# The last layer norm of a two-layer trunk: GpSimd arithmetic taken out, half of one scaling given to TensorE, six held weight units in place of five

## The chip, the cores and the metric

The kernel runs on one core of one Trainium2 chip. The metric is the device time in microseconds (us) of one execution; a lower time is better.

## The reference, cut to what matters

The reference is a decoder trunk of two layers over 256 tokens of width 2048, in float32. Each layer is a mixer (several kinds of attention), a layer norm, a squared-ReLU MLP and a second layer norm. Only the very end matters here: the second matrix of the last MLP, the residual sum and the last layer norm, whose result is the output.

```python
def layer_norm(x, g, b):
    mu = jnp.mean(xf, axis=-1, keepdims=True)
    xc = xf - mu
    var = jnp.mean(xc * xc, axis=-1, keepdims=True)
    y = xc * lax.rsqrt(var + LN_EPS) * g + b
...
def sqrelu_mlp(x, w1, w2):
    hid = jax.nn.relu(jnp.einsum('bsd,df->bsf', x, w1))
    return jnp.einsum('bsf,fd->bsd', hid * hid, w2)
...
x = layer_norm(ALPHA * x + sqrelu_mlp(x, mlp_w1[layer], mlp_w2[layer]), ln2_g[layer], ln2_b[layer])
```

## The kernel before, in words

Nearly the whole run is one stream of weight units. A unit is 128 x 1024 float32 numbers (512 KB) that SyncE's queue loads from HBM; ScalarE casts it to a high part (`w_hi`, line 120) and VectorE subtracts that to get the low part (`w_lo`, line 121). TensorE multiplies both parts with the activations, three products for each 128 x 512 piece (lines 371 to 373). The order of work on each engine is the order in which the Python code issues it; no scheduler moves anything.

The 256 tokens lie as two groups of 128 partitions, t = 0 and t = 1, in the tile `x` (`x_res` in the trace), 2048 columns each. A function works on four column blocks c = 0 to 3 of 512.

`as_` computes one column block of an MLP's output for both token groups into two PSUM banks (`acc`). The last block of the last MLP is 8 units of 12 products each, 6 for either group. With `hold=5` the first three units are used for both groups at once, and the last five are held: TensorE first takes all five for t = 0 (30 products), which completes t = 0, and then all five again for t = 1. Four of the held units lie in the ring buffers of `w_hi` and `w_lo`; the last two units of the stream have tiles of their own (`end_hi`, `end_lo`).

`moments` adds the last block to `x` (line 558), takes the statistics of it on VectorE (`bn`, `mv`, `ve`: lines 560, 582, 569) and has GpSimd compute the reciprocal deviation `rs` as a power (line 571), for t = 0 and then for t = 1.

`final` is the last layer norm. `rows` (`gb_rows`) holds the gain and the bias, broadcast to all partitions. For each group it normalises blocks 0 and 2 on ScalarE (`(x - mean) * r`, as an affine function with the tile `nmr`), then multiplies with the gain and adds the bias in two further steps (`two`), the adds on GpSimd, the products on VectorE except one that GpSimd has too. Blocks 1 and 3 are done by VectorE alone, in two fused steps of three operands each (`one`, lines 654 and 655). Each finished block goes to HBM from SyncE's queue, 256 KB each, eight in all.

Of the kernel before, what the change touches and what calls it, by code (L numbers as in the profile page):

```python
# [11 lines left out]
F32 = mybir.dt.float32  # L12
F32R = mybir.dt.float32r
BF16 = mybir.dt.bfloat16
AF = mybir.ActivationFunctionType
ALU = mybir.AluOpType
AX = mybir.AxisListType

P = 128
# [144 lines left out]
class Trunk:  # L164
# [479 lines left out]

    def final(self, last, stats):

        nc = self.nc
        rows = self.rows
        ov = self.a["out"][0].rearrange("(t p) d -> p t d", p=P)

        def one(t, c, mv, r):
            cs = slice(c * 512, (c + 1) * 512)
            xb = self.x[:, t, cs]
            nc.vector.scalar_tensor_tensor(xb, xb, mv[:, 0:1], rows[:, 0, cs], op0=ALU.subtract, op1=ALU.mult)
            nc.vector.scalar_tensor_tensor(xb, xb, r[:, 0:1], rows[:, 1, cs], op0=ALU.mult, op1=ALU.add)
            nc.sync.dma_start(ov[:, t, cs], xb)

        def two(t, c, op):
            cs = slice(c * 512, (c + 1) * 512)
            xb = self.x[:, t, cs]  # L660
            if op == ALU.mult:
                (nc.vector if t or c else nc.gpsimd).tensor_tensor(xb, xb, rows[:, 0, cs], op=op)
            else:
                nc.gpsimd.tensor_tensor(xb, xb, rows[:, 1, cs], op=op)
                nc.sync.dma_start(ov[:, t, cs], xb)

        for t, (mv, r) in enumerate(self.moments(last, stats)):
            nm = self.small.tile([P, 1], F32, name="nmr")
            nc.vector.scalar_tensor_tensor(nm, mv[:, 0:1], -1.0, r[:, 0:1], op0=ALU.mult, op1=ALU.mult)
            for c in (0, 2):  # L670
                xb = self.x[:, t, c * 512:(c + 1) * 512]
                nc.scalar.activation(xb, xb, AF.Identity, bias=nm, scale=r[:, 0:1])
            one(t, 1, mv, r)
            two(t, 0, ALU.mult)
            two(t, 0, ALU.add)
            two(t, 2, ALU.mult)
            two(t, 2, ALU.add)
            one(t, 3, mv, r)


    def qk(self, sc, q, k):
# [389 lines left out]
    def mlp(self, layer):  # L1071
        nc = self.nc
        st = self.new_stats()
        for q in range(4):
            hs = []
            cur = {}

            def take(f, bank):
                if f % 2 == 0:
                    cur["r"] = self.mp.tile([P, 512], F32, name="relu", bufs=3)  # L1080
                r = cur["r"]
                self.join(r[:, (f % 2) * S:(f % 2) * S + S], bank)
                if f % 2 == 0:
                    return
                sq = self.mp.tile([P, 512], F32, name="sq", bufs=2)
                hh = self.mp.tile([P, 512], F32R, name="h_hi", bufs=12)
                hl = self.mp.tile([P, 512], F32R, name="h_lo", bufs=12)

                def square():
                    nc.scalar.activation(r, r, AF.Relu)  # L1090
                    nc.scalar.activation(hh, r, AF.Square)
                    nc.vector.tensor_tensor(sq, r, r, op=ALU.mult)
                    nc.vector.tensor_tensor(hl, sq, hh.bitcast(F32), op=ALU.subtract)

                self.late.append(square)
                for j in range(2):
                    hs.append((hh[:, j * S:(j + 1) * S], hl[:, j * S:(j + 1) * S], None))

            for b in range(4):
                self.ws(self.xT, KT, 512, take, more=b % 2 == 1)  # L1100
                self.pump()
            self.finish_side()
            if layer == DEPTH - 1 and q == 0:
                self.rows = self.gb_rows(2, layer)
            for c in range(4):
                end = q == 3 and c == 3
                o = self.as_(hs, 16, 512, hold=(5 if layer else 2) if end else 0)
                if not end:
                    self.add_res(o, c, q == 0, st if q == 3 else None)
        return (o, c, False), st  # L1110
# [54 lines left out]
```

## Time and profile before

| What | us |
|---|---|
| median of 3 runs | 2243.89 |
| lowest and highest of them | 2241.61, 2249.12 |
| the profiled execution, its own time | 2248.41 |
| span of the profiled execution, first to last instruction | 2246.6 |

The span is what the trace shows; the profiled execution's own time is 1.81 us longer than its span. In the trace PE is TensorE, PEld its weight loads, DVE VectorE, ACT ScalarE, POOL GpSimd, and SPq the queue on which SyncE issues transfers. All times inside the trace count from the start of the span.

### The profile page before, as it was taken

What the parts mean: (1) busy time and instruction counts of PE and PEld (TensorE: products, weight loads), DVE (VectorE), ACT (ScalarE), POOL (GpSimd) and SP (SyncE); (2) the same over time, 40 slices, a digit from 0 to 9 for tenths busy, and PEclk for the clock granted to TensorE, in tenths of its full rate; (3) what the DMA queues carried; (4) which work ended last, traced back from release to release, by engine and by line L of the source; (5) the groups of instructions that cost most, each with busy time, mean ns of one, the idle gap of its engine ahead of it and who ended that gap; (6) DMA issues with size and microseconds to landing.
All of it is one profiled execution on the core that took longest, in us unless ns stands there. A gap on an engine that the chain in (4) does not pass through costs nothing.

```text
span 2246.6 us, 30036 instructions
## 1 busy us (share of the span) xinstructions
PE 2216.6 (99%) x11604; PEld 1847.6 (82%) x11604; DVE 1406.8 (63%) x1903; ACT 1060.7 (47%) x1525; POOL 62.0 (3%) x85
## 2 busy tenths in 40 slices
PE   9999999999999999999999999999999999999997
PEld 7878887788888888888878887778888888888885
DVE  5766355776556456556567887978555655554655
ACT  4554344454345345345344575635434534444542
POOL 0000000000000000000003201000000000000001
PEclk9999999999999999999999999999999999999998
DMA  7444454555655556565658443455656556555652
GB/s 266 145 118 147 131 168 141 189 178 193 191 187 188 190 176 200 193 188 170 206 161 226 154 136 127 148 184 184 227 194 189 178 198 189 186 194 181 194 190 104
DMA packets 224320, 399.07 MB, mean 178 GB/s; under 512 B 12778, under 2 KB 56512, under 8 KB 223408
## 3 DMA queue, kind: packets, MB, share of 16 engines
q1 hardware_dynamic: 221760, 387.30, 54.2%
q0 software_dynamic: 2416, 9.84, 1.6%
q8 instruction: 91, 1.49, 0.3%
q14 instruction: 53, 0.43, 0.1%
HBM read 395.00 MB, written 2.10 MB: 177 GB/s over the span
## 4 chain that ended last, share of the span: by engine, by line
PE 64%; issue 30%; DVE 4%; ACT 1%; DMA 1%; POOL 0%; SPq 0%; POOLq 0%; DVEq 0%; ACTq 0%
PE acc L325 14%; PE acc L371 9%; PE acc L373 9%; PE acc L372 9%; PE acc L326 7%; PE sc L325 3%; PE sc L326 2%; PE o L325 2%; PE pt L325 2%; PE pt L259 1%; PE o L278 1%; PE sc L685 1%; DVE w_lo L121 1%; PE sc L684 1%; PE o L326 1%
## 5 line engine op out<-in xcount | busy, mean ns | idle before, releaser
L121 DVE TENSOR_TENSOR w_lo<-raw,w_hi 128x1024 fp32r<-128x1024 f32 (+2 forms) x748 | 891.5, 1204 | 600.0 <-ACT w_hi L120 595.0
L120 ACT CAST w_hi<-raw 128x1024 fp32r<-128x1024 f32 (+2 forms) x748 | 759.9, 1029 | 770.2 <-PE acc L373 460.9
L325 PE MATMUL acc<-x,w_hi 128*128 128x512 f32 x1824 | 654.0, 402 | 4.3 <-DVE x L514 4.0
L326 PE MATMUL acc<-x,w_lo 128*128 128x256 f32 x1824 | 512.3, 281 | 0.6 <-DVE w_lo L121 0.6
L325 PEld LDWEIGHTS acc<-x,w_hi 128*128 128x128 f32 x1824 | 343.3, 188 | 94.4 <-issue 6.6
L373 PE MATMUL acc<-w_hi,h_lo 128*128 128x512 f32 x1016 | 400.3, 394 | 0.0
L372 PE MATMUL acc<-w_lo,h_hi 128*128 128x512 f32 x1016 | 398.2, 392 | 0.0
L371 PE MATMUL acc<-w_hi,h_hi 128*128 128x512 f32 x1016 | 394.4, 388 | 0.0
L326 PEld LDWEIGHTS acc<-x,w_lo 128*128 128x128 f32 x1824 | 345.2, 189 | 1.4 <-DVE w_lo L121 0.9
L372 PEld LDWEIGHTS acc<-w_lo,h_hi 128*128 128x128 f32 x1016 | 190.7, 188 | 44.3
L371 PEld LDWEIGHTS acc<-w_hi,h_hi 128*128 128x128 f32 x1016 | 190.7, 188 | 42.7
L373 PEld LDWEIGHTS acc<-w_hi,h_lo 128*128 128x128 f32 x1016 | 191.0, 188 | 38.1
L325 PE MATMUL sc<-x,w_hi 128*128 128x512 f32 x512 | 186.7, 399 | 0.0
L326 PE MATMUL sc<-x,w_lo 128*128 128x256 f32 x512 | 143.8, 281 | 0.0
L371 PE MATMUL acc<-w_hi,x 128*128 128x256 f32 (+2 forms) x400 | 136.4, 341 | 0.3 <-DVE x L513 0.2
L373 PE MATMUL acc<-w_hi,x 128*128 128x256 f32 (+2 forms) x400 | 132.5, 331 | 0.0
L372 PE MATMUL acc<-w_lo,x 128*128 128x256 f32 (+2 forms) x400 | 132.4, 331 | 0.0
L325 PEld LDWEIGHTS sc<-x,w_hi 128*128 128x128 f32 x512 | 96.2, 188 | 23.9
L337 ACT ACTIVATE xfull<-acc 128x256 f32<-128x256 f32 x130 | 49.6, 383 | 126.2 <-PE acc L326 108.7
L326 PEld LDWEIGHTS sc<-x,w_lo 128*128 128x128 f32 x512 | 96.7, 189 | 0.0
L325 PE MATMUL o<-x,w_hi 128*128 128x512 f32 x256 | 96.3, 399 | 0.0
L325 PE MATMUL pt<-x,w_hi 128*128 128x512 f32 x256 | 96.2, 399 | 0.0
(203 smaller groups left out, 2163.9 us busy)
## 6 DMA issues: line engine op xcount, KB each, us to landing
raw<-in_mlp_w SPq DMA_DIRECT2D x512, 512.0 KB, 4.2
raw<-in_even_w_in SPq DMA_DIRECT2D x92, 512.0 KB, 4.4
raw<-in_odd_w_in SPq DMA_DIRECT2D x56, 512.0 KB, 4.1
raw<-in_odd_w_out SPq DMA_DIRECT2D x32, 512.0 KB, 3.7
raw<-in_even_w_out SPq DMA_DIRECT2D x24, 512.0 KB, 3.7
gb_rows<-in_ln_g POOLq DMA_DIRECT2D x3, 1024.0 KB, 5.0
gb_rows<-in_ln_b POOLq DMA_DIRECT2D x3, 1024.0 KB, 7.1
raw<-in_odd_w_uq SPq DMA_DIRECT2D x8, 384.0 KB, 4.7
```

Of the source, the lines that this page charges most:

```text
L120: nc.scalar.copy(h, r)
L121: nc.vector.tensor_tensor(l, r, h.bitcast(F32), op=ALU.subtract)
L259: nc.tensor.transpose(pt[:, b * P:(b + 1) * P], st[:, u * 384 + b * P:u * 384 + (b + 1) * P], self.ident)
L278: nc.tensor.matmul(o[rows, :], v, w[:, 0:S], start=first, stop=False, skip_group_check=True)
L325: nc.tensor.matmul(banks[f], hi[:, c:c + P], both, start=first, stop=False, skip_group_check=True)
L326: nc.tensor.matmul(banks[f][:, S:2 * S], lo[:, c:c + P], xh, start=False, stop=last, skip_group_check=True)
L337: nc.scalar.activation(t, bank[:, S:2 * S], AF.Copy, scale=scale)
L371: nc.tensor.matmul(outs[t], xh[:, ts], hi[:, c:c + width], start=first, stop=False, skip_group_check=True)
L372: nc.tensor.matmul(outs[t], xh[:, ts], lo[:, c:c + width], start=False, stop=False, skip_group_check=True)
L373: nc.tensor.matmul(outs[t], xl[:, ts], hi[:, c:c + width], start=False, stop=last, skip_group_check=True)
L684: nc.tensor.matmul(sc[:, 0:P], q[:, 0:P], k[:, 0:P], start=True, stop=True, skip_group_check=True)
L685: nc.tensor.matmul(sc[:, P:384], q[:, P:S], k, start=True, stop=True, skip_group_check=True)
```

## The change

`final` is written anew, and `hold` is 6 for the last block. GpSimd keeps only the power for `rs`. For t = 0 all four blocks are done by VectorE in two fused steps, `centre` (subtract the mean, multiply with the gain) and `scale` (multiply with `r`, add the bias). For t = 1 blocks 2 and 3 are done the same way. Blocks 0 and 1 of t = 1 are centred by VectorE, and the scaling is a product on TensorE: ScalarE makes a diagonal matrix `dr` (tile name `g_row`) of `r`, one product with the identity puts the bias into a PSUM bank, a second with `dr` adds the scaled block, ScalarE copies the bank back and issues the transfer from its own queue. All operands of these products are float32.

```diff
-        for t, (mv, r) in enumerate(self.moments(last, stats)):
-            nm = self.small.tile([P, 1], F32, name="nmr")
-            nc.vector.scalar_tensor_tensor(nm, mv[:, 0:1], -1.0, r[:, 0:1], op0=ALU.mult, op1=ALU.mult)
-            for c in (0, 2):
-                xb = self.x[:, t, c * 512:(c + 1) * 512]
-                nc.scalar.activation(xb, xb, AF.Identity, bias=nm, scale=r[:, 0:1])
-            one(t, 1, mv, r)
-            two(t, 0, ALU.mult)
-            two(t, 0, ALU.add)
-            two(t, 2, ALU.mult)
-            two(t, 2, ALU.add)
-            one(t, 3, mv, r)
+        def centre(t, c, mv):
+            xb, _, g, _ = cut(t, c)
+            nc.vector.scalar_tensor_tensor(xb, xb, mv[:, 0:1], g, op0=ALU.subtract, op1=ALU.mult)
+
+        def scale(t, c, r):
+            xb, o, _, b = cut(t, c)
+            nc.vector.scalar_tensor_tensor(xb, xb, r[:, 0:1], b, op0=ALU.mult, op1=ALU.add)
+            nc.sync.dma_start(o, xb)
+
+        banks = [self.ps.tile([P, 512], F32, name=n) for n in ("pt", "o")]
+        dr = self.small.tile([P, P], F32, name="g_row", bufs=3)
+        for t, (mv, r) in enumerate(self.moments(last, stats)):
+            if t:
+                nc.scalar.activation(dr, self.ident, AF.Copy, scale=r[:, 0:1])
+                for c, bank in enumerate(banks):
+                    nc.tensor.matmul(bank, self.ident, cut(t, c)[3], start=True, stop=False, skip_group_check=True)
+            centre(t, 0, mv)
+            centre(t, 1, mv)
+            for c in range(2):
+                if t:
+                    xb, o, _, _ = cut(t, c)
+                    nc.tensor.matmul(banks[c], dr, xb, start=False, stop=True, skip_group_check=True)
+                    nc.scalar.copy(xb, banks[c])
+                    nc.scalar.dma_start(o, xb)
+                else:
+                    scale(t, c, r)
+            for c in range(2, 4):
+                centre(t, c, mv)
+                scale(t, c, r)
...
-                o = self.as_(hs, 16, 512, hold=(5 if layer else 2) if end else 0)
+                o = self.as_(hs, 16, 512, hold=(6 if layer else 2) if end else 0)
```

VectorE's order for t = 1, from the statistics to the program's end, was this (line 558 adds the last block, 662 is the gain of `two`, 654 and 655 are `one`):

```order
L558 TENSOR_TENSOR x_res<-x_res,acc 128x512 [waits PE_49]
L560 BN_STATS bn_13460<-x_res 128x6 [waits DVE_49]
L582 BN_AGGR mv<-bn_13460 128x2 [waits DVE_49]
L569 TENSOR_SCALAR ve<-mv 128x1 [waits DVE_49]
L669 SCALAR_TENSOR_TENSOR nmr<-mv,rs 128x1 [waits Pool_49]
L654 SCALAR_TENSOR_TENSOR x_res<-x_res,mv,gb_rows 128x512
L655 SCALAR_TENSOR_TENSOR x_res<-x_res,rs,gb_rows 128x512 [waits DVE_49]
L662 TENSOR_TENSOR x_res<-x_res,gb_rows 128x512 [waits Activation_49] x2
L654 SCALAR_TENSOR_TENSOR x_res<-x_res,mv,gb_rows 128x512
L655 SCALAR_TENSOR_TENSOR x_res<-x_res,rs,gb_rows 128x512 [waits DVE_49]
```

After the change the same stretch reads as below; line 658 is `centre`, line 662 is now `scale`:

```order
L558 TENSOR_TENSOR x_res<-x_res,acc 128x512 [waits PE_49]
L560 BN_STATS bn_13460<-x_res 128x6 [waits DVE_49]
L582 BN_AGGR mv<-bn_13460 128x2 [waits DVE_49]
L569 TENSOR_SCALAR ve<-mv 128x1 [waits DVE_49]
L658 SCALAR_TENSOR_TENSOR x_res<-x_res,mv,gb_rows 128x512 x3
L662 SCALAR_TENSOR_TENSOR x_res<-x_res,rs,gb_rows 128x512 [waits DVE_49,Pool_49]
L658 SCALAR_TENSOR_TENSOR x_res<-x_res,mv,gb_rows 128x512
L662 SCALAR_TENSOR_TENSOR x_res<-x_res,rs,gb_rows 128x512 [waits DVE_49]
```

Three `centre` steps now stand between the statistics and the first wait for GpSimd (`Pool_49`), and no step waits for ScalarE any more.

ScalarE's rows behind its last cast, at the program's end, are these after the change (`g_row` is `dr`, `pt` and `o` are the two PSUM banks):

```order
L120 CAST end_hi<-raw 128x1024 [waits DMAHW3_49]
L669 ACTIVATE g_row<-ident,rs 128x128 [waits DMASW5_49,DMASW3_49,DMASW7_49,DMASW1_49,Pool_49]
L678 COPY x_res<-pt 128x512 [waits PE_49]
L679 DMA out<-x_res 128x512 [waits Activation_49]
L678 COPY x_res<-o 128x512 [waits PE_49]
L679 DMA out<-x_res 128x512 [waits Activation_49]
```

The copy of the second bank stands behind the first transfer's issue; before, four affine steps (line 672) stood here, two for each group, and no transfer.

TensorE's end differs as follows; the four new rows are the bias products (line 671) and the products with `dr` (line 677):

```order
 L372 MATMUL acc<-end_lo,h_hi 128x512
 L373 MATMUL acc<-end_hi,h_lo 128x512
-L1161 UNCONDITIONAL_BRANCH
+L671 MATMUL pt<-gb_rows,ident 128x512
+L671 MATMUL o<-gb_rows,ident 128x512
+L677 MATMUL pt<-x_res,g_row 128x512
+L677 MATMUL o<-x_res,g_row 128x512
+L1167 UNCONDITIONAL_BRANCH
```

They follow the last product of t = 1. Further up, six products of t = 1 have moved from in front of t = 0's last 30 products to behind them; nothing else moves on TensorE.

## Rows read from the trace of the kernel before

**Rows 1.** The page: span, then busy time and share of each engine.

```profile
span 2246.6 us, 30036 instructions
PE 2216.6 (99%) x11604; PEld 1847.6 (82%) x11604; DVE 1406.8 (63%) x1903; ACT 1060.7 (47%) x1525; POOL 62.0 (3%) x85
```

**Rows 2.** Timeline of TensorE: start, duration, line, operation; last products of either group.

```profile
2223.96 0.39 PE L373 MATMUL acc<-end_hi,h_lo 128*128 128x512 f32 x1
...
2230.87 0.39 PE L373 MATMUL acc<-end_hi,h_lo 128*128 128x512 f32 x1
```

**Rows 3.** Timeline of VectorE from the last block's sum to the end.

```profile
2224.39 0.69 DVE L558 TENSOR_TENSOR x_res<-x_res,acc 128x512 f32<-128x512 f32 x1 [5.03 <-PE acc L373]
...
2226.14 0.15 DVE L569 TENSOR_SCALAR ve<-mv 128x1 f32<-128x1 f32 x1
...
2230.21 1.77 DVE L654 SCALAR_TENSOR_TENSOR x_res<-x_res,mv,gb_rows 128x512 f32<-128x512 f32 x1
...
2233.57 0.68 DVE L558 TENSOR_TENSOR x_res<-x_res,acc 128x512 f32<-128x512 f32 x1
...
2236.20 0.75 DVE L654 SCALAR_TENSOR_TENSOR x_res<-x_res,mv,gb_rows 128x512 f32<-128x512 f32 x1
2236.98 0.75 DVE L655 SCALAR_TENSOR_TENSOR x_res<-x_res,rs,gb_rows 128x512 f32<-128x512 f32 x1
2237.65 1.28 DVE L662 TENSOR_TENSOR x_res<-x_res,gb_rows 128x512 f32<-128x512 f32 x2
...
2240.64 1.63 DVE L655 SCALAR_TENSOR_TENSOR x_res<-x_res,rs,gb_rows 128x512 f32<-128x512 f32 x1
```

**Rows 4.** Timeline of GpSimd in the same stretch.

```profile
2229.82 3.29 POOL L664 TENSOR_TENSOR x_res<-x_res,gb_rows 128x512 f32<-128x512 f32 x2
2235.54 0.55 POOL L571 TENSOR_TENSOR rs<-ve,mhalf 128x1 f32<-128x1 f32 x1 [2.44 <-DVE ve L569]
```

**Rows 5.** Timeline of SyncE's queue: the last transfer's issue.

```profile
2242.30 0.33 SPq L656 DMA_DIRECT2D out<-x_res  x1
```

**Rows 6.** Windows: stretch, length, busy time of each engine, granted TensorE clock, DMA share, GB/s.

```profile
2242.50:2244.10 1.60, 0.00 (x0) 0.00 (x0) 0.00 (x0) 0.00 (x0) 0.00 (x0) 0.50 0.85 328
...
5.30:8.60 3.30, 1.64 (x12) 1.14 (x11) 2.44 (x4) 2.21 (x3) 0.40 (x1) 1.00 1.02 356
8.70:12.00 3.30, 3.30 (x12) 2.83 (x12) 1.97 (x3) 0.99 (x1) 0.00 (x0) 0.50 1.01 395
...
2231.30:2234.10 2.80, 0.00 (x0) 0.00 (x0) 2.76 (x3) 0.00 (x0) 1.80 (x2) 1.00 0.28 110
2234.20:2246.60 12.40, 0.00 (x0) 0.00 (x0) 7.23 (x11) 1.52 (x2) 3.85 (x3) 0.50 0.31 121
```

**Rows 7.** Timeline of VectorE: the last two units' low parts.

```profile
2217.01 2.35 DVE L121 TENSOR_TENSOR end_lo<-raw,end_hi 128x1024 fp32r<-128x1024 f32 x2
```

**Rows 8.** Timeline of TensorE at 74.5 us: one float32 product of 256 columns.

```profile
74.96 0.59 PE L685 MATMUL sc<-qk 64*128 64x256 f32 x2
```

**Rows 9.** Timeline of VectorE and GpSimd at 428 us, an earlier layer norm.

```profile
428.13 0.15 DVE L569 TENSOR_SCALAR ve<-mv 128x1 f32<-128x1 f32 x1
428.20 1.00 DVE L598 TENSOR_SCALAR x_res<-x_res,mv,rs 128x512 f32<-128x512 f32 x2
...
428.37 0.86 POOL L571 TENSOR_TENSOR rs<-ve,mhalf 128x1 f32<-128x1 f32 x1 [2.17 <-DVE ve L569]
```

**Rows 10.** Groups of ScalarE's instructions by shape: count, busy us, mean ns.

```profile
L711 ACT ACTIVATE S<-S,nm 128x128 f32<-128x128 f32 x32 | 12.9, 404 | 11.1 <-DVE nm L704 7.7 <-DVE nm L702 3.3
...
L507 ACT COPY xfull<-sc 128x512 f32<-128x512 f32 x8 | 4.7, 582 | 4.1 <-PE sc L501 4.1
```

**Rows 11.** Transfers: queue, count, KB each, median us from issue to landing.

```profile
gb_rows<-in_ln_b POOLq DMA_DIRECT2D x3, 1024.0 KB, 7.1
...
out<-x_res SPq DMA_DIRECT2D x8, 256.0 KB, 2.0
...
ident<-in_ident SPq DMA_DIRECT2D x1, 64.0 KB, 1.9
```

More of the change, by code (lines that the diff above doesn't have):

```diff
@@ L649, in final, with cut @@
         ov = self.a["out"][0].rearrange("(t p) d -> p t d", p=P)
-        def one(t, c, mv, r):
+        def cut(t, c):
             cs = slice(c * 512, (c + 1) * 512)
[L653 to L665, printed above, removed]
@@ L667, in final @@
-        for t, (mv, r) in enumerate(self.moments(last, stats)):
-            nm = self.small.tile([P, 1], F32, name="nmr")
-            nc.vector.scalar_tensor_tensor(nm, mv[:, 0:1], -1.0, r[:, 0:1], op0=ALU.mult, op1=ALU.mult)
-            for c in (0, 2):
-                xb = self.x[:, t, c * 512:(c + 1) * 512]
-                nc.scalar.activation(xb, xb, AF.Identity, bias=nm, scale=r[:, 0:1])
-            one(t, 1, mv, r)
-            two(t, 0, ALU.mult)
-            two(t, 0, ALU.add)
-            two(t, 2, ALU.mult)
-            two(t, 2, ALU.add)
-            one(t, 3, mv, r)
+            return self.x[:, t, cs], ov[:, t, cs], rows[:, 0, cs], rows[:, 1, cs]
```

## The prediction

> **What bounds the kernel now.** I read the page first. TensorE is busy for 99% of the span [rows 1], so up to its last product the time is TensorE's, and the change leaves the number of those products alone. What it can win or lose lies in the tail behind them, so the second view is the timeline of that tail, engine by engine. TensorE's last product for t = 0 ends at 2223.96 + 0.39 = 2224.35 and its last for t = 1 at 2230.87 + 0.39 = 2231.26 [rows 2]; the span ends at 2246.6. The tail is 15.3 us.
>
> VectorE fills it. It starts t = 0 at 2224.39, 0.04 after TensorE, but starts t = 1 only at 2233.57, 2.27 us after it could (2231.26 + 0.04 = 2231.30), because it is still busy with t = 0 [rows 3]. It ends at 2240.64 + 1.63 = 2242.27, and the last transfer is issued at 2242.30 [rows 5]. From there to the end of the span are 4.30 us, of which 2.0 are the landing [rows 11]. I keep what follows the landing.
>
> Why it is slow shows in two rows beside each other. The same fused step takes 0.75 us at 2236.20 and 2236.98, with GpSimd idle, and 1.77 at 2230.21 and 1.63 at 2240.64 [rows 3]. GpSimd's two adds run from 2229.82 to 2233.11, 1.65 each [rows 4]: the first ends at 2231.47, and VectorE's slow step ends 0.51 later, at 2231.98. VectorE stood still until GpSimd was done. That is the cost the change can take away.
>
> **The held units.** Thirty products lie between the two rows of group 2: 6.91 / 30 = 0.23 us each. With six held units, six products of t = 1 go behind t = 0, so t = 0 is complete 6 x 0.23 = 1.37 us earlier, and t = 1 ends when it did. The price is supply: in t = 0's pass a unit now lasts 1.37 us where the first of them lasted 2.75. The pass starts at 2231.26 less its drain and 72 products, at 2214.5, and comes to the last unit at 2221.4; that unit's low part is ready at 2217.01 + 2.35 = 2219.36 [rows 7], 2 us ahead. Its order on ScalarE and VectorE does not change. I cost this edit at nothing; a shortage would be paid one to one.
>
> **VectorE, t = 0.** It starts at 2224.39 - 1.37 = 2223.02. The statistics take 2226.14 - 2224.39 = 1.75 to `ve`; a step that waits for nothing starts 0.07 behind `ve` [rows 9]. A dependent fused step follows 0.78 behind its predecessor, an independent one 0.67 (2236.20, 2236.98, 2237.65 [rows 3]). Eight steps, two of them directly dependent: 1.82 + 5 x 0.67 + 2 x 0.78 + 0.75 = 7.48, so they end at 2230.50, 0.8 before TensorE delivers t = 1. The eight steps are therefore hidden by TensorE. With five held units they would end at 2231.87 and cost 0.57; that is what the sixth unit is worth here.
>
> **VectorE, t = 1.** It starts at 2231.30, a gain of 2.27. Six fused steps: 1.82 + 3 x 0.67 + 2 x 0.78 + 0.75 = 6.14, where before it took 2242.27 - 2233.57 = 8.70: a gain of 2.56. Its last issue comes at 2231.30 + 6.14 + 0.03 = 2237.47, against 2242.30: **-4.83**.
>
> **The other branch, t = 1.** `ve` starts at 2233.05, GpSimd 0.23 later (2235.31 and 2235.54 [rows 4]). How long `rs` takes beside VectorE's `centre` steps is not shown directly. Alone it takes 0.55 [rows 4]. Beside two VectorE steps that followed each other it took 0.86 and ended at 429.23, 0.03 after the second of them [rows 9]. So it ends at the end of a VectorE step: the first `centre` (0.82 behind `ve`, so `rs` at 2233.90), or at worst the third (2235.24). I take the first, since in rows 9 the first step it could have followed ended near 428.7 (two steps in 1.00), 0.2 before `rs` would have been done alone (428.92), so `rs` had to wait for the second; here the first step ends 0.04 after that point. Then `dr`, nearest row 0.40 [rows 10], is ready at 2234.34.
>
> The products are float32. A row of 256 columns shows two instructions and 0.59 us in all, 0.38 for one, so they follow 0.21 apart [rows 8], 512 columns then 0.43 apart: 1.02 for the first product, 0.85 more for the second. The bias products wait for nothing late and run from 2231.26 to about 2233.0, under the statistics. The products with `dr` end at 2235.40 and 2236.25. A copy of 512 columns out of PSUM takes 0.58 [rows 10], an issue 0.33 [rows 5]; copies end at 2236.02 and 2236.96, and ScalarE's last issue is at 2237.0. That is 0.5 before VectorE's, so this branch is hidden by VectorE.
>
> **Transfers.** Before, the last 512 KB, two transfers, moved between 2242.50 and 2244.10 at 328 GB/s [rows 6]: 0.75 to 0.8 each, done 1.8 behind the last issue. Now four are issued within 1.5 us, from 2236.05 to 2237.47. The first starts to move about 0.9 behind its issue (estimate: 1.8 less one transfer and a little queueing); four end at 2236.95 + 4 x 0.75 = 2239.95, 2.5 behind the last issue. I add **0.6**; the bounds are 0 and 0.7.
>
> **Sum.** -4.83 + 0.6 = -4.2. The profiled execution would take 2248.4 - 4.2 = 2244.2; it lies 4.5 above the median of the runs, and against that median of 2243.89 the forecast is **2239.7**, 0.19% less.
>
> **Rivals.** (1) `rs` waits for all three `centre` steps, at 2235.24. Then `dr` is at 2235.68, the products end at 2236.74 and 2237.59, and ScalarE's last issue is at 2238.3, 0.8 behind VectorE's. Its transfer queues behind two others and ends 2.2 behind its issue: -4.0 + 0.4 = -3.6, so 2240.3. For it: rows 9. Against: at 2230.21 GpSimd got its turn although VectorE's next step had started 0.1 earlier [rows 3, 4]. The Trainium skill, page "SBUF — State Buffer", section "Who interferes with whom", says that a VectorE instruction with two SBUF inputs and a GpSimd instruction that reads SBUF block each other wholly, whichever starts first. The slow rows of groups 3 and 4 agree, and read strictly it would give this rival's 2240.3.
>
> (2) TensorE runs the products with `dr` at half clock. In this trace the clock was still granted in full for 2.8 us after the last product and was 0.50 from 2234.2 on [rows 6]; that is 1.2 GHz in place of 2.4. Now TensorE stops at about 2233.0 and goes on at 2234.38, after 1.4 us, so I expect full clock. But at the start it fell to 0.50 after a stretch in which TensorE was busy for 1.64 of 3.30 us [rows 6]. At half clock the products take 1.87 and 1.71, ScalarE's last issue is at 2238.6: -3.8, 2240.1. With (1) as well: issue at 2239.9, 2241.4. The Trainium skill, page "TensorE: Matmul & The Clock Gate", Part 1, calls the half clock the state of an idle array, which speaks against giving late, lone work to TensorE; the rows at 2234.2 agree.
>
> (3) The other side: ScalarE's queue has issued nothing in this trace. Landing is 2.0 from SyncE's queue, whose first transfer showed nothing special at 1.9, but 7.1 from GpSimd's [rows 11], for four times the size. ScalarE's last issue at 2237.0 makes the kernel slower than before once its landing takes more than 2242.30 + 2.0 - 2237.0 = 7.3. At twice GpSimd's, 14.2, the time is 2250.8.
>
> (4) The change doesn't do what it says: supply of the sixth unit falls short. At 2 us of room it takes a shortage of 6.2 to undo the gain, and at 8 the time is 2245.7. Nothing in rows 7 points to it.
>
> **Chances.** Forecast 0.65; (1) or (2) alone 0.18, both 0.07; (3) 0.04; (4) 0.02; something unseen 0.04. By their mechanism all but the last three give between 2239 and 2241.5. The three runs shown lie from 2.3 below to 5.2 above their median, and a median of new runs has its share of that; so the range is **2236.0 to 2244.0**. About 0.3% (6.7 us) is what a measurement of this kernel can tell from no change. The forecast is inside it; the scatter alone can carry it out on the fast side: faster 0.18, same 0.77, slower 0.05.
>
> **What would show it.** Right: VectorE's sum for t = 0 starts 1.4 earlier against TensorE's last product, eight fused steps of 0.75 without one of 1.6, its sum for t = 1 starts 0.04 behind TensorE, the last SyncE issue stands 6.2 behind that. `rs` of t = 1 lasts about 0.6; if 1.3 or 1.9, (1) holds. Float32 products 0.43 apart show full clock, 0.85 half. ScalarE's transfers land in 2 to 3 us. The forecast is wrong if VectorE's steps stay at 1.6 with GpSimd idle, if TensorE gains waits in the last 17 us, or if the span after the last issue is far from 4.9.

## The result, and the profile after

| | before | changed |
|---|---|---|
| median of 7 runs each, us | 2243.89 | 2251.63 |
| lowest and highest | 2241.61, 2249.12 | 2251.4, 2254.83 |
| profiled execution, its span | 2246.6 | 2251.1 |

The ratio is 1.0035, with a 95% interval of 1.0023 to 1.0046: the change made the kernel 0.35% slower, where the forecast was 0.19% faster. The measured median lies 7.6 us above the top of the forecast's range.

The page still gives TensorE 99% of the span.

```profile
span 2251.1 us, 30043 instructions
PE 2229.0 (99%) x11611; PEld 1845.7 (82%) x11612; DVE 1404.3 (62%) x1904; ACT 1059.2 (47%) x1524; POOL 54.7 (2%) x80
```

The tail comes first, since the forecast was made there. The timeline of TensorE, to set against [rows 2]:

```profile
2240.24 0.39 PE L373 MATMUL acc<-end_hi,h_lo 128*128 128x512 f32 x1
2240.47 1.02 PE L671 MATMUL pt<-gb_rows,ident 128*128 128x512 f32 x2
...
2244.12 1.13 PE L677 MATMUL pt<-x_res,g_row 128*128 128x512 f32 x2 [1.77 <-ACT g_row L669]
2245.08 1.02 PE L677 MATMUL o<-x_res,g_row 128*128 128x512 f32 x2
```

VectorE of the same stretch, to set against [rows 3]:

```profile
2232.32 0.69 DVE L558 TENSOR_TENSOR x_res<-x_res,acc 128x512 f32<-128x512 f32 x1 [3.74 <-PE acc L373]
...
2239.01 0.75 DVE L662 SCALAR_TENSOR_TENSOR x_res<-x_res,rs,gb_rows 128x512 f32<-128x512 f32 x1
2240.67 0.69 DVE L558 TENSOR_TENSOR x_res<-x_res,acc 128x512 f32<-128x512 f32 x1 [0.90 <-PE acc L373]
...
2242.41 0.15 DVE L569 TENSOR_SCALAR ve<-mv 128x1 f32<-128x1 f32 x1
2242.48 2.07 DVE L658 SCALAR_TENSOR_TENSOR x_res<-x_res,mv,gb_rows 128x512 f32<-128x512 f32 x3
...
2246.10 0.75 DVE L662 SCALAR_TENSOR_TENSOR x_res<-x_res,rs,gb_rows 128x512 f32<-128x512 f32 x1
```

GpSimd, ScalarE and SyncE's queue there ([rows 4, 5]):

```profile
2242.64 0.99 POOL L571 TENSOR_TENSOR rs<-ve,mhalf 128x1 f32<-128x1 f32 x1 [7.34 <-DVE ve L569]
...
2243.66 0.40 ACT L669 ACTIVATE g_row<-ident,rs 128x128 f32<-128x128 f32 x1 [16.73 <-POOL rs L571]
...
2246.32 0.59 ACT L678 COPY x_res<-o 128x512 f32<-128x512 f32 x1 [0.45 <-PE o L677]
2246.93 0.35 ACTq L679 DMA_DIRECT2D out<-x_res  x1
...
2236.23 10.98 SPq L663 DMA_DIRECT2D out<-x_res  x6
```

Now set the starts of TensorE's last MLP product, L373 into the t = 1 bank, beside each other. From it to the end of the span were 2246.6 - 2230.87 = 15.73 us before, and are 2251.1 - 2240.24 = 10.86 now. **The tail is 4.87 us shorter, and everything ahead of it is 9.37 us longer.** I call these two parts the tail and the stream.

Where the stream lost is read from windows that lie wholly inside one kind of product. A window counts each product that touches it. These products last 0.39 to 0.40, so in 40 us the count is about 40.39 divided by the distance from one start to the next. First the kernel before: two windows in products of L371 to L373 whose weights are the MLP's hidden tiles `h_hi` and `h_lo`, then two in the first matrix's products (`ws`, L325 and L326, in turn 512 and 256 columns wide). A line gives the stretch, its length, TensorE's busy time with the count, the granted clock, the share of the DMA engines' time and GB/s.

```profile
720.00:760.00 40.00, 40.00 (x177) 1.00 0.59 195
2000.00:2040.00 40.00, 40.00 (x176) 1.00 0.58 188
640.00:680.00 40.00, 40.00 (x229) 1.00 0.63 197
820.00:860.00 40.00, 40.00 (x228) 1.00 0.65 206
```

The changed kernel, the same windows:

```profile
720.00:760.00 40.00, 40.00 (x173) 1.00 0.56 195
2000.00:2040.00 40.00, 40.00 (x173) 1.00 0.53 187
640.00:680.00 40.00, 40.00 (x228) 1.00 0.58 184
820.00:860.00 40.00, 40.00 (x233) 1.00 0.58 188
```

TensorE is busy for all of each window and the granted clock is 1.00 (2.4 GHz) in both kernels, yet 173 products fit where 176 to 177 did. Taken over all starts, the distance is 228.9 ns before and 233.3 after, alike in every block of both MLPs. No row shows a wait. 3072 such products (2 layers x 4 x 4 blocks x 16 x 2 x 3) at 4.4 ns make 13.5 us, and the attention's output products, whose weights are the tile `y`, 432 in the trace, another 1.1 (106.5 us in all before, 107.5 now). Part of that came back in other products: in the first matrix's products the mean distance is 176.7 or 173.3 ns, one or the other for a whole stretch of some 512 products. In this trace three of the eight stretches ran at the shorter one (the window at 820 is in one of them), in that of before none: 3 x 512 x 3.4 ns = 5.2 us. 13.5 + 1.1 - 5.2 = 9.4, for the 9.37 that the two rows differ.

Nothing in the diff touches these products. But the diff removes a tile. `nmr` had five buffers of 32 bytes in each partition, at the end of the pool of small tiles, and all tiles that are allocated after it moved 160 bytes down. In the two compiled programs they start at:

```
tile      before   beyond a multiple of 256   changed   beyond it
w_hi       42240     0                          42240      0
h_hi      159936   192                         159776     32
h_lo      184512   192                         184352     32
y         202432   192                         202272     32
end_hi    209088   192                         208928     32
```

**Theory one:** the distance hangs on where the weights' tiles (`h`, `y`) lie. **Theory two:** it hangs on something else in the change, such as the held units, the instructions or the queues.

### The profile page after: what moved, and what is told of

It reads as the page before. It is cut to its first block, busy times and chain, and to the rows that moved or that the text cites. A ratio compares the mean times of both kernels' runs of the same rounds, so it can differ in the third digit from the quotient of the medians.

```text
span 2251.1 us, 30043 instructions
## 1 busy us (share of the span) xinstructions
PE 2229.0 (99%) x11611; PEld 1845.7 (82%) x11612; DVE 1404.3 (62%) x1904; ACT 1059.2 (47%) x1524; POOL 54.7 (2%) x80
## 4 chain that ended last, share of the span: by engine, by line
PE 92%; DVE 3%; issue 1%; DMA 1%; ACT 1%; POOL 0%; SPq 0%; POOLq 0%; ACTq 0%; DVEq 0%
PE acc L325 18%; PE acc L371 14%; PE acc L372 14%; PE acc L373 14%; PE acc L326 9%; PE sc L325 5%; PE sc L326 3%; PE pt L325 3%; PE o L325 3%; PE o L326 1%; PE pt L326 1%; PE pt L259 1%; DVE w_lo L121 1%; PE o L278 1%; PE sc L691 1%
## 5 line engine op out<-in xcount | busy, mean ns | idle before, releaser
L325 PE MATMUL acc<-x,w_hi 128*128 128x512 f32 x1824 | 650.3, 400 | 4.7 <-DVE x L514 4.4
L326 PE MATMUL acc<-x,w_lo 128*128 128x256 f32 x1824 | 510.1, 280 | 0.5 <-DVE w_lo L121 0.5
L325 PEld LDWEIGHTS acc<-x,w_hi 128*128 128x128 f32 x1824 | 342.4, 188 | 93.7 <-issue 6.2
L373 PE MATMUL acc<-w_hi,h_lo 128*128 128x512 f32 x1016 | 401.9, 396 | 0.0
L371 PE MATMUL acc<-w_hi,h_hi 128*128 128x512 f32 x1016 | 401.8, 396 | 0.0
L326 PEld LDWEIGHTS acc<-x,w_lo 128*128 128x128 f32 x1824 | 344.0, 189 | 1.3 <-DVE w_lo L121 0.8
L371 PEld LDWEIGHTS acc<-w_hi,h_hi 128*128 128x128 f32 x1016 | 190.9, 188 | 46.3
L373 PEld LDWEIGHTS acc<-w_hi,h_lo 128*128 128x128 f32 x1016 | 190.9, 188 | 46.0
L325 PE MATMUL sc<-x,w_hi 128*128 128x512 f32 x512 | 185.6, 397 | 0.0
L326 PE MATMUL sc<-x,w_lo 128*128 128x256 f32 x512 | 143.0, 279 | 0.0
L371 PE MATMUL acc<-w_hi,x 128*128 128x256 f32 (+2 forms) x400 | 136.4, 341 | 0.3 <-DVE x L513 0.2
L373 PE MATMUL acc<-w_hi,x 128*128 128x256 f32 (+2 forms) x400 | 132.5, 331 | 0.0
L325 PEld LDWEIGHTS sc<-x,w_hi 128*128 128x128 f32 x512 | 96.1, 188 | 23.4
L326 PEld LDWEIGHTS sc<-x,w_lo 128*128 128x128 f32 x512 | 96.5, 188 | 0.0
L325 PE MATMUL pt<-x,w_hi 128*128 128x512 f32 x256 | 95.8, 397 | 0.0
L325 PE MATMUL o<-x,w_hi 128*128 128x512 f32 x256 | 95.7, 397 | 0.0
```

The costliest lines, as they stand in the source:

```text
L325: nc.tensor.matmul(banks[f], hi[:, c:c + P], both, start=first, stop=False, skip_group_check=True)
L326: nc.tensor.matmul(banks[f][:, S:2 * S], lo[:, c:c + P], xh, start=False, stop=last, skip_group_check=True)
L371: nc.tensor.matmul(outs[t], xh[:, ts], hi[:, c:c + width], start=first, stop=False, skip_group_check=True)
L373: nc.tensor.matmul(outs[t], xl[:, ts], hi[:, c:c + width], start=False, stop=last, skip_group_check=True)
```

## The experiments

Times are medians; the ratio is to the kernel before, run in turn on the same chip; chips differ from one set of runs to the next (the kernel before has medians of 2243.89 to 2246.56), so times of different sets are best compared by their ratios. The distance is the mean from one start to the next over all h-fed products of the trace (those whose weights are `h_hi` or `h_lo`; y-fed are those with `y`), and the tail is counted as above.

### Back to the old places, and away from them

e1, in the changed kernel:

```diff
+        self.small.tile([P, 1], F32, name="pad", bufs=5)
         banks = [self.ps.tile([P, 512], F32, name=n) for n in ("pt", "o")]
```

> The changed kernel with an unused tile of 160 bytes per partition put where the removed one was, so that every later tile, h_hi, h_lo and y among them, stands at its old address; nothing else differs. Theory one (TensorE's pace hangs on the address of the tile that it loads as weights: a multiple of 64 bytes before, 32 beyond one after): the h-fed products come back from 233.3 ns apart to 229, the last one starts near 2231 instead of 2240.2, the tail of 10.5 us stays, and the time is 2239 to 2240 us, 4 to 5 below the kernel before. Theory two (the pace hangs on something else in the change: held units, queues, instructions, the chip): still 233.3 ns and 2251.6 us.

e2, in the kernel before (the column comes out of a buffer that is there anyway):

```diff
-            nm = self.small.tile([P, 1], F32, name="nmr")
+            nm = self.small.tile([P, 2], F32, name="ve")[:, 0:1]
```

> The kernel before with the removed tile's column taken from another tile, so that the later tiles move by the same 160 bytes and nothing else changes. Theory one: the h-fed products go from 229 to 233.3 ns apart, the last one starts 9.4 us later, near 2240, and the time is 2253 us, or up to 2257 if all 3072 products lose 4.4 ns with nothing given back. Theory two: 229 ns and 2243.9 us as before.

Measured: e1 2240.04 us against 2245.83, ratio 0.9975 (0.9967 to 0.9984). e2 2258.52 against 2245.83, ratio 1.0061 (1.0047 to 1.0075). Windows of e1, then of e2, and e2's last product:

```profile
720.00:760.00 40.00, 40.00 (x176) 1.00 0.58 192
2000.00:2040.00 40.00, 40.00 (x176) 1.00 0.60 189
```

```profile
720.00:760.00 40.00, 40.00 (x173) 1.00 0.56 186
2000.00:2040.00 40.00, 40.00 (x173) 1.00 0.58 190
...
2239.70 0.39 PE L373 MATMUL acc<-end_hi,h_lo 128*128 128x512 f32 x1
```

With the old places the changed kernel is back at 228.9 ns; with the new places the kernel before goes to 233.3, and its last product starts 8.8 us later than before, with its old tail of 15.7 (span 2255.4). Its median is 12.7 us above the kernel before, between the 9 and the 13 that were expected above a kernel before of 2243.9. Theory two falls: 160 unused bytes decide it, whatever the rest of the change does. The forecast for the tail stands too: e1's is 2238.1 - 2227.20 = 10.9 us, as in the changed kernel. That its time of 2240.04 is so near the forecast of 2239.7 is partly luck: the kernel before was 1.9 us slower in this set of runs, and in e1's trace two `ws` stretches ran at the shorter distance (2 x 512 x 3.4 ns = 3.5 us), so that its last product starts at 2227.20 and not near 2231.

### Which places are good

e3, e4 and e8 are e1 with `bufs=1`, `2` and `3`, so that all later tiles start 64, 96 and 128 beyond a multiple of 256.

> The changed kernel with an unused tile of 32 bytes, so that the later tiles start at multiples of 64 bytes, though not at their old addresses. Theory one in its form 'a multiple of 64 is enough': 229 ns apart and 2239 to 2240 us. If the exact old place counts and not the multiple, or by theory two: 233.3 ns and 2251.6 us.

> The changed kernel with an unused tile of 64 bytes, so that the later tiles stand 32 bytes beyond a multiple of 64 again, at other addresses than in the changed kernel. Theory one: 233.3 ns apart and 2251 to 2252 us, as changed. If any shift of the tiles mends it: 229 ns and 2239 to 2240 us. Theory two: 2251.6 us, so this run tells theory one from 'any other place' and not from theory two.

> The changed kernel with an unused tile of 96 bytes, so that all later tiles start 64 bytes below their old places: h_hi, h_lo and y at multiples of 128 that are not multiples of 256. If multiples of 128 are the good case for a weight tile: 229 ns or less and 2239 to 2240 us. If only the old residue, 192 beyond a multiple of 256, is good: 233 to 234 ns and 2247 to 2254 us.

Measured: e3 233.3 ns, 2247.36 us (ratio 1.0011, 1.0002 to 1.0021); e4 234.3 ns, 2254.21 (1.0039, 1.0025 to 1.0053); e8 232.4 ns, 2250.8 (1.0023, 1.0013 to 1.0032). So multiples of 64 or of 128 bytes are not enough, and my first form of theory one was wrong. e3 is 4 us faster than the changed kernel at the same 233.3 ns; in its trace seven of the eight `ws` stretches ran at the shorter distance, against three.

The next runs move `h_hi` and `h_lo` alone, by gaps in their own pool. e6 and e7 are e1 with a gap of 64 or 256 bytes:

```diff
+                if q == 0 and f == 1:
+                    self.mp.tile([P, 16], F32, name="gap")
                 hh = self.mp.tile([P, 512], F32R, name="h_hi", bufs=12)
```

e5 is the kernel before with such a gap of 96 bytes between `h_hi` and `h_lo`; e11, e12 and e13 are e1 with gaps ahead of `h_hi` and between the two (64 and 192, 96 and 160, 0 and 64 bytes).

> The kernel before with an unused tile of 96 bytes between the h_hi and the h_lo tiles: only h_lo (and the end tiles) move, to 32 beyond a multiple of 256, where the changed kernel has them; h_hi, y and all else stay. If the place of the tile that is loaded as weights decides: one product in three (L373) is slower, so the h-fed stream goes from 228.9 to a mean between 230 and 232 ns, and the time rises by 3 to 6 us, to 2247 to 2252. If it is the place of other tiles that moved along (relu, sq, y, the layer norm's rows): 228.9 ns and no change, 2244 to 2246 us.

> The changed kernel with the old addresses (160-byte pad) and a gap of 64 bytes ahead of h_hi, so that h_hi and h_lo start at multiples of 256 (before: 192 beyond one); y and all else at the old places. If the start within 256 bytes decides, 192 was fast and 32, 64 and 96 slow, so 0 may be either: 229 ns or less and 2239 to 2240 us if multiples of 256 are the good case, or 233 to 234 ns and 2247 to 2252 us if 192 is the only one. If the weights' place has no part in it: 228.9 ns and 2240 us.

> As the run with a 64-byte gap, with 256 bytes: h_hi and h_lo start 192 beyond a multiple of 256 as before, at other addresses. If the start within 256 bytes decides: 228.9 ns and 2240 us. If the distance to other tiles, or the exact place, decides: 233 ns and 2247 to 2252 us.

> The changed kernel with the old addresses and h_hi alone moved by 64 bytes to a multiple of 256; h_lo and the end tiles move by 256 bytes and so stay 192 beyond one. If h_hi alone decides (h_lo's move of 96 bytes had changed nothing): 226.7 ns and 2236 to 2237 us. If both count: 228 ns and 2238 us.

> As the run before it, with h_hi 96 bytes up, at 32 beyond a multiple of 256, where the changed kernel has it, and h_lo at 192 as before. If h_hi alone decides: 233.3 ns and 2246 to 2252 us, though h_lo is where it was in the kernel before. If h_lo counts: between 229 and 233 ns.

> The changed kernel with the old addresses and a gap of 64 bytes between h_hi and h_lo: h_hi 192 beyond a multiple of 256 as in the kernel before, h_lo (and the end tiles) at 0. If h_lo's place has no part while h_hi is at 192: 228.9 ns and 2239 to 2240 us, as with h_lo at 192 and at 32. If a product is slow whenever its weight tile and the one before it start at different places: about 231 ns, as with h_hi at 0 and h_lo at 192.

e9 is the changed kernel with `ss` in 4 buffers, which brings every later tile to a multiple of 256; e10 is e9 with 64 bytes put in front of everything, so that `w_hi` and `w_lo` move with the rest.

```diff
-        ss = self.small.tile([P, 2], F32, name="ss")
+        ss = self.small.tile([P, 2], F32, name="ss", bufs=4)
...
+        const.tile([P, 16], F32, name="pad")
         self.ident = const.tile([P, P], F32, name="ident")
```

> The changed kernel with one buffer of 32 bytes less in the pool of the small tiles (ss with 4 instead of 5), so that all later tiles start at multiples of 256: h_hi, h_lo, end_hi, y and the layer norm's rows; w_hi and x do so already. If the start of the h tiles within 256 bytes decides, the h-fed products are 226.7 ns apart as with the 64-byte gap, the y-fed ones go from 229.5 to about 227, and the time is 2236 to 2237 us. If the old addresses of y or of the rows had a part in the good runs: above 2240.

> The kernel with all tiles at multiples of 256, and 64 bytes put in front of everything, so that weights (h) and moving tiles (w_hi, w_lo) both start 64 beyond a multiple of 256. If the start of the weight tile by itself decides, as in the run with h at 64 and w at 0: 233.3 ns and 2247 to 2252 us. If the distance of the weight tile from the moving tile within 256 bytes decides: it is 0 here, 226.7 ns and 2236 to 2238 us.

All of them in one table, bytes beyond a multiple of 256:

| h_hi | h_lo | w_hi, w_lo | distance, ns | kernels (median us, ratio to before) |
|---|---|---|---|---|
| 0 | 0 | 0 | 226.7 | e6 (2236.92, 0.9962), e9 (2236.58, 0.9958) |
| 64 | 64 | 64 | 226.7 | e10 (2236.3, 0.9959) |
| 192 | 192 | 0 | 228.9 | before, e1, e7 (2240.49, 0.9977) |
| 192 | 32 | 0 | 228.9 | e5 (2248.38, 1.0011) |
| 192 | 0 | 0 | 228.9 | e13 (2235.68, 0.9963) |
| 0 | 192 | 0 | 231.1 | e11 (2239.3, 0.9969) |
| 128 | 128 | 0 | 232.4 | e8 |
| 32 | 192 | 0 | 232.6 | e12 (2248.71, 1.001) |
| 32 | 32 | 0 | 233.3 | changed, e2 |
| 64 | 64 | 0 | 233.3 | e3 |
| 96 | 96 | 0 | 234.3 | e4 |

Windows of e9, of e10 and of e11 (h-fed, h-fed, `ws`, `ws`; e9's are the first two alone):

```profile
720.00:760.00 40.00, 40.00 (x178) 1.00 0.57 194
2000.00:2040.00 40.00, 40.00 (x178) 1.00 0.59 191
```

```profile
720.00:760.00 40.00, 40.00 (x179) 1.00 0.56 192
2000.00:2040.00 40.00, 40.00 (x179) 1.00 0.61 195
640.00:680.00 40.00, 40.00 (x229) 1.00 0.64 201
820.00:860.00 40.00, 40.00 (x229) 1.00 0.66 203
```

```profile
720.00:760.00 40.00, 40.00 (x175) 1.00 0.57 192
2000.00:2040.00 40.00, 40.00 (x174) 1.00 0.57 186
640.00:680.00 40.00, 40.00 (x233) 1.00 0.67 207
820.00:860.00 40.00, 40.00 (x232) 1.00 0.64 203
```

What follows:
- A move by 256 bytes changes nothing (e7), so it is the start within 256 bytes that counts, at least for the moves tried here.
- The same 64 is slow beside moving tiles at 0 (e3, 233.3) and as good as any beside moving tiles at 64 (e10, 226.7). So the place of the weight tile by itself does not decide; the place against other tiles does. e10 moved all other tiles as well, but every trace also varies the moving tile alone: the last two units have the tiles `end_hi` and `end_lo`, which start where `h_lo` does within 256 bytes. In the changed kernel that is 32, like the weights, and in t = 0's pass six steps beside `w` at 0 take 1.40 us (233 ns each), the next eleven beside the end tiles 2.50 (227):

```profile
2227.99 0.40 PE L371 MATMUL acc<-w_hi,h_hi 128*128 128x512 f32 x1
...
2229.39 0.40 PE L371 MATMUL acc<-end_hi,h_hi 128*128 128x512 f32 x1
...
2231.89 0.39 PE L373 MATMUL acc<-end_hi,h_lo 128*128 128x512 f32 x1
```

- In t = 1's pass the same products are 229 ns apart. In e5, with the weights where they are, the products beside the end tiles (at 32) are 232 ns apart and those beside `w` (at 0) 228.9. The moving tile's place counts.
- "h_hi alone decides" fell with e11: with `h_hi` at 0, `h_lo` at 192 costs 4.4 ns. But with `h_hi` at 192, `h_lo` is free (e5, e13). The second of the three products loads the same weights as the first, the third loads the others; how the three add up to these distances I can't say, and no run settles it.
- Over the whole stream, equal places are the best case found: against the kernel before, e6, e9 and e10 are 0.38 to 0.42% faster, tail included. It is no law: in the kernel before the end tiles and both weight tiles are at 192, and there the two passes of twelve products are 229.0 and 231.3 ns apart, no better than beside `w` at 0. The y-fed products, which e9 was expected to speed up by 2.5 ns, gained 1 (106.0 us for 432, 106.5 before).
- A time of a whole run is a poor measure of this: e13 is as fast as e10 at 2.2 ns more, and e11 is only 3 us above e10 at 4.4 ns more. In e11 all eight `ws` stretches ran at the shorter distance (233 and 232 in a window, against 229), which is 8 x 512 x 3.4 ns = 13.9 us given back; e10 has two such stretches, e13 five. e5 is slower than the kernel before by ratio at the same 228.9 ns; in its trace no stretch ran at the shorter one.

### Places and tail together

e17 is the kernel before with the 64-byte gap of e6.

> The kernel before with a gap of 64 bytes ahead of h_hi, so that h_hi, h_lo and the end tiles start at multiples of 256 like w_hi; its tail as it was. If places and tail add up: 226.7 ns instead of 228.9 for 3072 products, 6.8 us less in the stream, 2238 to 2240 us where the kernel before has 2244 to 2246, and a tail of 15.7 us. If the gain of the places belongs to the changed kernel only: no difference from before.

Measured: 226.7 ns, last product at 2225.05 where it was 2230.87, a tail of 2240.9 - 2225.05 = 15.85 us, and 2241.18 us against 2246.02, ratio 0.9979 (0.997 to 0.9988). No `ws` stretch ran at the shorter distance in either trace, so 5.8 us are the places alone. Summed over the trace, the h-fed products took 6.7 us less, as worked out (6.8), and the others 0.9 more. Places and tail add up.

### The parts of the tail

e14 is e1 with `scale` for blocks 0 and 1 of t = 1 on VectorE, without `dr`, the four products and the copies; e15 is e1 and e16 the kernel before with the other number of held units.

```diff
...
-                if t:
-                    xb, o, _, _ = cut(t, c)
-                    nc.tensor.matmul(banks[c], dr, xb, start=False, stop=True, skip_group_check=True)
-                    nc.scalar.copy(xb, banks[c])
-                    nc.scalar.dma_start(o, xb)
-                else:
-                    scale(t, c, r)
+                scale(t, c, r)
```

```diff
-                o = self.as_(hs, 16, 512, hold=(6 if layer else 2) if end else 0)
+                o = self.as_(hs, 16, 512, hold=(5 if layer else 2) if end else 0)
```

> The changed kernel with the old addresses, and without the products with the diagonal matrix: for t=1 all four centres and all four scalings are on VectorE, as for t=0. By the forecast's working two scalings of 0.75 us come back into VectorE's row, so its last instruction ends 1.5 us later behind t=1's sum, and the tail from the start of TensorE's last MLP product to the end goes from 10.9 to 12.3 us; time 2241 to 2242 us, the stream at 228.9 ns. If ScalarE's two transfers, which are issued last now, are what ends the kernel: less than 1.5, down to 0.9.

> The changed kernel with the old addresses and five held units as before. By the forecast's working t=0's part then starts 1.37 us later against TensorE's last product, VectorE ends t=0 about 0.5 us after t=1's sum could start, and the tail goes from 10.9 to 11.4 us; time 0.5 above that of six units, too little for the clock on the wall, so the rows decide. If six units cost TensorE anything: the start of its last product is earlier here than with six.

> The kernel before with six held units and nothing else. Its t=1 sum started 2.3 us after TensorE's last product, held up by t=0's work on VectorE; with t=0 1.37 us earlier it starts 0.9 behind, and the tail goes from 15.7 to 14.3 us; time 2244 to 2245 where the kernel before has 2246, stream at 228.9 ns. If the sixth unit delays TensorE: no gain.

| kernel | last product | span | tail, us | median, ratio |
|---|---|---|---|---|
| e1 | 2227.20 | 2238.1 | 10.9 | 2240.04, 0.9975 |
| e14, all scaling on VectorE | 2228.18 | 2239.3 | 11.1 | 2239.57, 0.9979 |
| e15, five held units | 2228.21 | 2240.3 | 12.1 | 2240.61, 0.9983 |
| before | 2230.87 | 2246.6 | 15.7 | |
| e16, before with six | 2225.46 | 2239.8 | 14.3 | 2243.61, 0.9999 |

**e16** came out as expected, 1.4 us of tail, though its time can't be told from the kernel before.

**e14** lost only 0.2 us of tail where 1.5 or 0.9 were expected. The last rows of e1, then of e14:

```profile
2233.84 0.33 SPq L663 DMA_DIRECT2D out<-x_res  x1
2233.90 0.35 ACTq L680 DMA_DIRECT2D out<-x_res  x1
```

```profile
2235.30 0.75 DVE L662 SCALAR_TENSOR_TENSOR x_res<-x_res,rs,gb_rows 128x512 f32<-128x512 f32 x1
2236.08 0.33 SPq L663 DMA_DIRECT2D out<-x_res  x1
...
2236.80:2237.70 0.90, 0.00 (x0) 0.00 (x0) 0.00 (x0) 0.00 (x0) 0.00 (x0) 0.50 0.81 300
2237.70:2239.30 1.60, 0.00 (x0) 0.00 (x0) 0.00 (x0) 0.00 (x0) 0.00 (x0) 0.50 0.00 0
```

Behind its last product, e1 issues last after 6.70 us and e14 after 7.90, so the products with the diagonal matrix do bring the last issue 1.2 us forward. But e1 has 4.2 us from there to the end and e14 only 3.2. e1's last four transfers are issued close together and end 2.2 behind the last issue, while e14's last one moves alone and ends 1.6 behind it; what follows is 1.9 in e1 and 1.6 in e14. The changed kernel's own windows show the same: its last four transfers, from VectorE's 2245.40 to 2246.93 in their issue, move in one stretch of 2.95 us at 356 GB/s, which ends 2.2 behind the last issue, at 2249.15. The third line is the kernel before, from the end of its last transfer:

```profile
2246.20:2249.15 2.95, 0.00 (x0) 0.00 (x0) 0.65 (x1) 0.59 (x1) 0.00 (x0) 0.91 0.92 356
2249.15:2251.10 1.95, 0.00 (x0) 0.00 (x0) 0.00 (x0) 0.00 (x0) 0.00 (x0) 0.50 0.02 4
...
2244.03:2246.60 2.57, 0.00 (x0) 0.00 (x0) 0.00 (x0) 0.00 (x0) 0.00 (x0) 0.50 0.01 3
```

e18 is e14 with all tiles at multiples of 256 (as e9).

> The changed kernel with all later tiles at multiples of 256 and all of the scaling on VectorE, no product with a diagonal matrix. If places and tail add up: 226.7 ns, a tail of 11.1 us, 0.2 more than with the products, and a time of 2236 to 2237 us, not to be told from the 2236.6 with them. If the products are worth the 1.3 us by which they shorten VectorE's row: 2238.

Measured: 2236.87 us (ratio 0.996, 0.9946 to 0.9974), tail 2234.2 - 2223.03 = 11.2; e9 with the products had 2236.58 and 10.9. TensorE's share of the scaling is worth 0.2 to 0.3 us of the tail, the two times can't be told apart, and the simpler kernel is as fast.

**e15** cost 1.2 us of tail where 0.5 were expected. TensorE's timeline and windows of e15 (in these, the busy time of each engine, then the granted clock):

```profile
2232.54 1.78 PE L678 MATMUL pt<-x_res,g_row 128*128 128x512 f32 x2 [2.23 <-ACT g_row L670]
2234.11 1.92 PE L678 MATMUL o<-x_res,g_row 128*128 128x512 f32 x2
...
2232.00:2234.00 2.00, 1.46 (x2) 0.64 (x3) 1.90 (x4) 0.40 (x1) 0.05 (x1) 0.72 0.00 0
2234.00:2236.00 2.00, 2.00 (x3) 0.34 (x1) 1.24 (x2) 0.59 (x1) 0.00 (x0) 0.50 0.40 155
```

VectorE is late with t = 0 by 0.45, near the forecast. The rest is the clock, in this one trace. TensorE stands still for 2.23 us before the products with `dr`, where it is 1.77 in the changed kernel; here the granted clock falls to 0.50 (1.2 GHz) and the two products take 1.78 and 1.92 where they took 1.13 and 1.02. ScalarE's last issue then stands 7.59 behind t = 1's sum, against 6.27 in e1, and ends the kernel; its transfer ends 1.6 behind that issue where e1's ended 2.2 behind it, which gives 0.6 back. With six held units the products with `dr` ran at full clock in all twelve traces that have them. The Trainium skill, page "TensorE: Matmul & The Clock Gate", Part 1, gives the half clock as the state of an idle array; these rows agree. The kernel before kept the full clock for 2.8 us behind its last product [rows 6], so what makes it fall in e15 stays open.

## Why the prediction was wrong, point by point

**What bounds the kernel now: the step that failed.** "Up to its last product the time is TensorE's, and the change leaves the number of those products alone." The number was left alone; the distance from one to the next was not, and it went from 228.9 to 233.3 ns because a removed tile moved the tiles behind it. That is 9.37 us in the traces. e1 and e2 show that nothing else was needed. The forecast put nothing down for it: it took the pace of these products as given and named lost supply as the only way in which the stream could get longer. The order of instructions shows nothing of this; the compiled programs' tile places do. Why the places set the pace stays open.

**The held units: right, and mis-sized.** t = 0's sum starts 2240.24 - 2232.32 = 7.92 ahead of the last product, 6.48 before: 1.44 earlier, forecast 1.37. No shortage. The sixth unit is worth 1.2 in the changed kernel (e15), forecast 0.57: with five, the products with `dr` also ran at half clock. Whether they always do is not shown.

**VectorE, t = 0 and t = 1: right.** Eight steps end 7.44 behind the start (forecast 7.48), six end 6.18 behind it (6.14), t = 1's sum starts 0.04 behind TensorE, and no step of 1.6 is left. (That VectorE "stood still until GpSimd was done" fits the rows only roughly: its slow step ended 0.51 behind GpSimd's add, sooner than the 0.75 that the step takes alone.) The last SyncE issue is at 2236.23 + 10.98 - 0.33 = 2246.88, 6.21 behind t = 1's sum (6.2).

**The other branch: a term too small.** `rs` took 0.99, not 0.6, and ended 1.22 behind `ve`; I had 0.85 and at worst 2.19. It ended between the ends of the first `centre` (2243.22, from three steps in 2.07) and the second. Mostly for that, 0.37, and for a first product of 1.13 and not 1.02, ScalarE's last issue, at 2246.93, stands 0.05 behind SyncE's instead of 0.5 ahead.

**Transfers: the mechanism was right, its sum was not.** The four end 2.2 behind the last issue, where 2.5 was worked out. But the end of the span follows their end after 1.95 where it was 2.57 before, so the whole is 4.17 from the last issue, against 4.30 in the kernel before, and not 4.9. That last stretch is 1.6 in e14; I had kept it fixed.

**Sum.** Tail: -4.87 measured, -4.2 forecast. To the last issue it is 2246.93 - 2240.24 = 6.69 where it was 2242.30 - 2230.87 = 11.43, a gain of 4.74 (forecast 4.83); what follows is 0.13 shorter (forecast 0.6 longer). With the old places (e1) the time is 5.8 us under the kernel before, 4.8 of it in the tail.

**Rivals.** (1) fell, at least in its form: `rs` did not wait for the third `centre`. The reason given against it misread its rows: they have GpSimd's add start at 2229.82, ahead of VectorE's step at 2230.21 [rows 3, 4]. The Trainium skill, page "SBUF — State Buffer", section "Who interferes with whom", has the two engines block each other; the rows agree that `rs` is longer beside VectorE's steps (0.99 against 0.55 alone) and show no VectorE step that is longer for it. (2) did not happen in the changed kernel and did in e15. (3) and (4) did not happen: ScalarE's transfers landed in 2.4 us.

```profile
out<-x_res SPq DMA_DIRECT2D x6, 256.0 KB, 2.0
out<-x_res ACTq DMA_DIRECT2D x2, 256.0 KB, 2.4
```

The rival on the other side that did come true was not among those with a mechanism. It had a share of the 0.04 for "something unseen".

## What to carry to other kernels

Where an edit adds, removes or resizes a tile in a pool, compare the start of every later tile between the two compiled programs before pricing anything else: in a kernel that TensorE bounds for 99% of the span, 160 unused bytes moved the stream by 9 us in the traces (and e2's median by 12.7), twice what the intended edit won. A change of pace without a wait shows in no list of waits, only in the count of products in windows of equal length. Where weight tiles and moving tiles start at the same place within 256 bytes, this kernel was at its best: 0.2% under the kernel before by the places alone (e17), 0.4% with the shorter tail.

## What the runs showed of the hardware that I had not expected

- Products of 128 x 512 whose weights are loaded anew each time start 226.7 to 234.3 ns apart, at the granted clock of 1.00, according to where the weight tiles and the moving tiles lie. The Trainium skill, page "SBUF — State Buffer", section "Who interferes with whom", gives TensorE two independent read ports, one for the moving operand and one for the weights, and says that it never waits on anyone. No run here shows it waiting for another engine. But the distance differs by up to 7.6 ns a product when nothing but such places changes, so its pace is not independent of where they lie, and the measurement decides; whether the read ports are the cause is not shown.
- The `ws` products, in turn 512 and 256 columns wide, start 176.7 or 173.3 ns apart on average, one or the other for a whole stretch of some 512. Two kernels whose tiles lie alike within 256 bytes, e1 and e7, had the shorter one in the same two stretches of eight; the changed kernel and e2, which also lie alike, had it in different ones. The kernel before had it in none and e16, with the same places, in four, so the places alone do not choose it. What does stays open and was not tried. At the shorter one throughout, e10 would save another 6 x 512 x 3.4 ns = 10.4 us.
- The time from the end of the last transfer's movement to the end of the span is not fixed: 2.6 us in the five kernels with the old layer norm, 1.9 to 2.0 in the thirteen in which ScalarE's queue issues the last transfers, 1.6 in e14 and e18, where VectorE does all of the scaling and SyncE's queue issues all. What sets it stays open.
